# Weight splitting in a fused two-block transformer: one block per run of matmuls in the attention layers, and every low part issued one block behind its high part

## The chip, the cores and the metric

The kernel runs on one core of one Trainium2 chip. The metric is the time of one execution in device microseconds (us). Instructions of one engine run in the order in which they stand in that engine's queue; PE is TensorE (matmuls), DVE is VectorE, ACT is ScalarE, POOL is GpSimd, SP is the queue that issues most of the loads.

## What is computed

The reference runs two model blocks, one behind the other, on 256 tokens of width 1024 in fp32. Cut to what matters:

```python
def first_block(x, mem, ...):                    # two layers
    mem_n = rmsnorm(mem, mem_norm_g)
    for i in range(2):
        mem_k, mem_v = split(mem_n @ mem_w_kv[i])
        x = x + 0.5 * swiglu(rmsnorm(x, norm_g[i, 0]), ffn_w_up[i, 0], ffn_w_down[i, 0])
        h = rmsnorm(x, norm_g[i, 1])
        x = x + (pool_layer(h, ...) if i == 0 else diff_layer(h, ...))
        x = x + 0.5 * swiglu(rmsnorm(x, norm_g[i, 2]), ffn_w_up[i, 1], ffn_w_down[i, 1])
    return rmsnorm(x, final_norm_g)

def second_block(x, c, ...):                     # one layer
    mod = silu(c) @ w_ada + b_ada                # six vectors of shifts, scales and gates
    h = modulate(rms_norm(x, norm_attn), sh1, sc1)
    x = x + g1 * hybrid_mixer(h, w_in, w_out, rel_bias)   # MOBA heads and DSA heads (top-k select)
    h = modulate(rms_norm(x, norm_ffn), sh2, sc2)
    x = x + g2 * peer_ffn(h, w_query, sub_keys, u_emb, v_emb)   # 16384 experts, top 16 of 8 heads
    return rms_norm(x, norm_final)
```

`pool_layer` mixes moving averages with attention over `mem`; `diff_layer` is causal attention with the difference of two softmaxes, beside attention over `mem`.

## The kernel before, in words

**Products in three matmuls.** Each fp32 operand is split into a high part (rounded to the matmul's fp32r format) and a low part (the rest). A product is the sum of high x high (L184), high x low (L185) and low x high (L186), which `mm3` issues one after the other for each 128 rows of the inner dimension.

**Weights as a stream.** All weights come as 654 blocks of up to 512 KB, here counted 0 to 653 in the order in which they are used. For each block SP issues a load into a `raw` buffer (five buffers, later four), ACT copies it into `whi` (L144), and DVE subtracts into `wlo` (L145). In between lie items with a `call`: pieces of the matrix `w_ada`, which DVE adds up itself (`ada_piece`, the rows `acc` of L463 and L465) beside the feed-forward halves.

```python
    def split_one():
        j = st["split"]
        load_to(j + cfg["raw"])
        ...
            ACT.activation(hi[:, :n], r[:, :n], AF.Copy)
            V.tensor_tensor(lo[:, :n], r[:, :n], hi[:, :n].bitcast(F32), op=OP.subtract)
```

**When a block is split.** The tile framework's scheduler is off: the order of the program is the order of each engine. A group of matmuls begins with `fetch(4)`, which calls `nextw` for each of the four blocks that the group uses, and `nextw` splits until four blocks beyond the one that it hands out are split (`cfg["ahead"]` is 4; 2 for the experts). So the four blocks of the next group are split at the start of this one, in a row on ACT and on DVE.

**Where the blocks are used.** 0 to 15 are the keys and values of `mem`; 16 to 81, 108 to 173, 174 to 239 and 280 to 345 the four feed-forward halves (44 blocks up, 22 down); 82 to 107 the pool layer; 240 to 279 the diff layer; 346 to 381 the projections of MOBA and DSA; 382 to 397 the query projection of the experts, 398 to 653 the experts. In the up projections a group is 4 blocks by 96 matmuls of 128x256: the weights are stationary, and the first 24 matmuls go through all four blocks once, so the group meets its fourth block's low part at its 21st matmul.

**Layers with other work between.** In the attention layers generators are stepped in turn: `proj_cols`, `v_part` or `u_part` (one run of matmuls to a step), and units of attention, whose steps put softmax rows on DVE and ACT and small matmuls and transposes on PE. A table `counts` sets how many runs of matmuls follow each step. The output projection of the hybrid attention (`out_proj_k`) calls `fetch(4)` for blocks 382 to 385 and then `realT(0)`, which computes the modulation `ma` (L343), scales the transposed activations (`xg`, L355 and L353) and splits them into `hT` for the next projection.

Of the kernel before, what the change touches and what calls it, by code (L numbers as in the profile page):

```python
# [60 lines left out]
def kernel(ctx: ExitStack, tc: tile.TileContext, A, LAY, stop=None):  # L61
# [4 lines left out]
    def pool(name, bufs=1, **kw):  # L66
        return tc.tile_pool(name=name, bufs=bufs, reuse_waits="tile", **kw)
# [32 lines left out]


    items = []
    st = {"load": 0, "split": 0, "use": 0, "nsplit": 0, "raw": {}, "s": {}}
    deferred = []
    cfg = {"raw": 5, "ahead": 4}
    CH = 1024
    wpool = ctx.enter_context(pool("wp", side="right"))
    wstack = ctx.enter_context(ExitStack())
# [11 lines left out]
    def load_to(n):  # L120
        while st["load"] < min(n, len(items)):
            ap, nk, w = items[st["load"]][:3]
            if st["load"] < dense and st["load"] % 5 == 4:
                r = wpool2.tile([P, CH], F32, name="raw", tag="raw", bufs=1)
            else:
                r = wpool.tile([P, CH], F32, name="raw", tag="raw", bufs=4)
            nc.sync.dma_start(r[:, :nk * w], ap)
            st["raw"][st["load"]] = r
            st["load"] += 1

    def split_one():
        j = st["split"]
        load_to(j + cfg["raw"])
        _, nk, w, call = items[j][:4]
        n = nk * w
        r = st["raw"].pop(j)
        if call is not None:
            call(r[:, :n].rearrange("p (k w) -> p k w", w=w))
        else:
            p_ = wpool2 if j < dense and st["nsplit"] % 2 else wpool  # L140
            st["nsplit"] += 1
            hi = p_.tile([P, CH], F32R, name="whi", tag="whi", bufs=4)
            lo = p_.tile([P, CH], F32R, name="wlo", tag="wlo", bufs=4)
            ACT.activation(hi[:, :n], r[:, :n], AF.Copy)  # L144
            V.tensor_tensor(lo[:, :n], r[:, :n], hi[:, :n].bitcast(F32), op=OP.subtract)  # L145
            st["s"][j] = Split(hi[:, :n].rearrange("p (k w) -> p k w", w=w), lo[:, :n].rearrange("p (k w) -> p k w", w=w))
        st["split"] += 1
        load_to(j + 1 + cfg["raw"])

    def nextw():  # L150
        while items[st["use"]][3] is not None:
            st["use"] += 1
        j = st["use"]
        ahead, k = 0, j + 1
        while k < len(items) and ahead < cfg["ahead"]:
            ahead += items[k][3] is None
            k += 1
        while st["split"] < k:
            split_one()
        st["use"] += 1  # L160
        return st["s"].pop(j), items[j][1], items[j][2]

    def split_more(n):
        for _ in range(n):
# [12 lines left out]
    def run_deferred():  # L177
        while deferred:
            deferred.pop(0)()
        for f in strip_hook:  # L180
            f()
# [21 lines left out]
    def rows_mm(p, act, got, t, c0, w, K):  # L203
        for c, k, kt in got:
            mm3(p, act[:, kt, t * P:(t + 1) * P], c[:, k, c0:c0 + w], kt == 0, kt == K - 1)
# [18 lines left out]
    def proj_cols(act, n, n_ct, evac):  # L224
        got = fetch(n)
        for c0 in range(0, n_ct, 2):
            p = pmm()
            m = min(2, n_ct - c0)
            for j in range(m):
                if j:  # L230
                    yield
                proj_col(act, got, c0 + j, p[:, j * S:(j + 1) * S])
            evac(c0, m, p[:, :m * S].rearrange("p (j t) -> p j t", t=S))
            yield
        run_deferred()

    def drain(*gens):
        for g in gens:
            for _ in g:
                pass  # L240
# [153 lines left out]
    def out_proj_k(segs, update, nxt, tail=2, ahead=None):  # L394


        p = [[pmm() for _ in range(2)] for _ in range(NT)]
        n = len(segs)

        def mm(t, h, gis, gots):  # L400
            for gi in gis:
                act, k0 = segs[gi]
                for c, k, _ in gots[gi][h]:
                    mm3(p[t][h], act[:, k0 + k, t * P:(t + 1) * P], c[:, k, :], gi == 0 and k == 0, gi == n - 1 and k == 1)

        gots = {}
        for gi in range(n - tail):
            gots[gi] = [fetch(1), fetch(1)]
            for t in range(NT):
                for h in range(2):  # L410
                    mm(t, h, [gi], gots)
                if t:
                    run_deferred()
                yield
        was = dict(cfg)
        cfg.update(ahead=8 - 2 * tail)
        for gi in range(n - tail, n):
            gots[gi] = [fetch(1), fetch(1)]
        cfg.update(was)
        for t in range(NT):  # L420
            for h in range(2):
                cut = n - 1 if nxt.deep and t and h else n
                mm(t, h, range(n - tail, cut), gots)
                if cut < n:
                    was = dict(cfg)
                    cfg.update(ahead=0)
                    ahead.append(fetch(4))
                    nxt.realT(0)
                    mm(t, h, range(cut, n), gots)
                    if tail > 2:  # L430
                        split_more(1)
                update(t, h, p[t][h])
                nxt.pre(t, h)
                if not nxt.deep and (t or h):
                    nxt.T(*((0, 0), (0, 1), (1, 0))[2 * t + h - 1])
                if h:
                    nxt.stats(t)
                if cut < n:
                    ahead.append(fetch(4))
                    cfg.update(was)  # L440
                yield
        if not nxt.deep:
            nxt.late = [lambda: nxt.T(1, 1)]
# [306 lines left out]
        return dump(xt)  # L750

    n2 = Norm(A["norm_g"][0, 2])
    with pool("pl") as sp:
        cat = Split(sp.tile([P, 12, S], F32R, name="cat_hi"), sp.tile([P, 12, S], F32R, name="cat_lo"))
        pb = sp.tile([P, 4, 384], F32, name="poolB")
# [6 lines left out]
        def u_part(h):  # L762
            got = fetch(4)
            for t in range(NT):
                n1.before(t)
                p = pmm()
                rows_mm(p, hT, got[:4], t, 0, 512, 8)
                yield
                rows_mm(p, hT, got[4:], t, 0, 512, 8)
                ACT.activation(u[t][:, h * 512:(h + 1) * 512], p, AF.Copy, scale=n1.rstd[:, t:t + 1])  # L770
                if t:
                    run_deferred()
                yield

        def pooled(c0):
# [8 lines left out]
        def mixed():  # L784
            for c0 in range(0, 8, 2):
                pooled(c0)
                yield
            wg = fetch(2)
            for ct in range(8):
                g, db = ct // 2, ct % 2  # L790
                p = psm()[:, :S]
                for cb in range(2):
                    col = cb * S + db * P
                    mm3(p, wg[g][0][:, g % 2, col:col + P], hT[:, 2 * g + cb, :], cb == 0, cb == 1)
                split_evac(cat[:, ct, :], p, psc[:, ct:ct + 1])
                if ct % 2:
                    yield

        drain(u_part(0), proj_cols(hT, 4, 4, lambda c0, m, p: ACT.activation(qT[:, c0:c0 + m, :], p, AF.Copy)))
# [3 lines left out]
        for n, _ in zip(counts, pipeline(units, [(1, 2), (3, 3), (None, 0), (0, 0), (2, 2)])):  # L803
            for _ in range(n):
                step(fill)
        drain(fill)
    kv0.close()
    if stop == "pool":
        return dump(xt)
# [9 lines left out]


    n5 = Norm(A["norm_g"][1, 2])
    with pool("df") as sp:
        cat = Split(sp.tile([P, 12, S], F32R, name="cat_hi"), sp.tile([P, 12, S], F32R, name="cat_lo"))
        nd = sp.tile([P, S], F32, name="nd")
# [97 lines left out]
        def v_part(h):  # L922

            got = fetch(4)
            for t in range(NT):
                n4.before(t)
                p = pmm()
                rows_mm(p, hT, got[:4], t, 0, 512, 8)
                yield
                rows_mm(p, hT, got[4:], t, 0, 512, 8)  # L930
                ACT.activation(v[:, t, h * 512:(h + 1) * 512], p, AF.Copy, scale=n4.rstd[:, t:t + 1])
                if t:
                    run_deferred()
                yield

        drain(v_part(0))
# [12 lines left out]
        for i, _ in enumerate(pipeline(units, [(5, 6), (1, 2), (4, 4), (None, 0), (6, 6), (0, 0), (3, 3), (2, 2)])):  # L949
            for _ in range(counts[i] if i < len(counts) else 1):  # L950
                step(fill)
        drain(o)
    kv1.close()
    if stop == "diff":
        return dump(xt)
# [45 lines left out]
        return dump(xt)  # L1001


    gotv, got = m1.got
    mvp = [pmm() for _ in range(NT)]
    iqp, ixp = pmm(), psm()
# [93 lines left out]
    def v_part():  # L1100
        got = fetch(4)
        for t in range(NT):
            p = pmm()
            rows_mm(p, hT, got[:4], t, 0, 512, 8)
            yield
            rows_mm(p, hT, got[4:], t, 0, 512, 8)
            ACT.activation(av[:, t, 512:], p, AF.Copy)
            if t:
                run_deferred()
            yield  # L1110

    def make(t, g):
# [88 lines left out]
        return dump(xt)  # L1201


    got = m2.got
    def q_rows(b, t):
        p = pmm()
# [87 lines left out]
    for f in late_scores:  # L1294
        f()
    q1st.close()
    wstack.close()
    pq2 = pqst.enter_context(pool("pq2"))

# [335 lines left out]
```

## Time and profile before

| what | value |
|---|---|
| time, median of 3 runs | 2098.37 us (2098.26 to 2100.83) |
| the profiled execution: time, span of its instructions | 2098.71 us, 2096.9 us |
| mean granted clock of TensorE | 0.987 |
| PE busy | 2033.5 us, 97% of the span |
| DVE busy | 1458.4 us, 70% |
| ACT busy | 985.5 us, 47% |

The profile is of one execution. Busy time is the time in which an engine has an instruction under way; the granted clock is TensorE's clock as a share of its full 2.4 GHz. A row of the timeline gives the start and duration in us, the engine, the line, the operation, what is written `<-` what is read, the size, how many like instructions in a row (x4), and in brackets the idle time of the engine ahead of it with what ended it.

### The profile page before, as it was taken

The page shows a single profiled execution, that of the slowest core. Times are in us where ns is not written, and L with a number is a line of the kernel's source. Part 1 is how long each engine was busy: PE and PEld are TensorE (multiplying, and loading weights), DVE is VectorE, ACT ScalarE, POOL GpSimd, SP SyncE. Part 2 cuts the span into 40 slices and gives each one's busy share as a digit, 9 for nine tenths or more (in the row PEclk, how much of TensorE's full clock was granted, in tenths as well). Part 3 has the DMA queues.
Part 4 walks back from the last instruction along what each step waited for, and adds up shares of the span by engine and source line. Part 5 has one row for each costly group of instructions (what it writes and reads, how often), then busy time and mean ns, then how long its engine had stood idle before and what let it go on. Part 6 is the DMA issues. An engine that isn't in the chain of part 4 may idle for free. (4 is left out here: it accounts for less than half of the span.)

```text
span 2096.9 us, 34488 instructions
## 1 busy us (share of the span) xinstructions
PE 2033.5 (97%) x13678; PEld 1832.0 (87%) x13678; DVE 1458.4 (70%) x2330; ACT 985.5 (47%) x1508; POOL 39.0 (2%) x74
## 2 busy tenths in 40 slices
PE   8999999999999998899989899999999999999998
PEld 7999888998999797799878779999998888888886
DVE  6677566776677568756658688889976666666666
ACT  6444454444444445354444344455554444444444
POOL 2000000000000000000000000000000000000000
PEclk9999999999999999999999899999999999999999
DMA  7667535676576552355545333556676776777764
GB/s 274 217 236 266 188 134 205 227 250 233 185 248 244 187 195 101 120 191 198 206 124 180 104 98 134 175 178 213 245 252 209 226 231 207 225 243 225 225 211 140
DMA packets 142379, 416.93 MB, mean 199 GB/s; under 512 B 12469, under 2 KB 47429, under 8 KB 140041
## 3 DMA queue, kind: packets, MB, share of 16 engines
q1 hardware_dynamic: 102672, 372.04, 52.4%
q10 hardware_dynamic: 37976, 36.91, 5.5%
q0 software_dynamic: 1568, 5.77, 0.9%
q8 instruction: 107, 1.75, 0.3%
q14 instruction: 56, 0.45, 0.1%
HBM read 396.82 MB, written 17.86 MB: 198 GB/s over the span
## 5 line engine op out<-in xcount | busy, mean ns | idle before, releaser
L145 DVE TENSOR_TENSOR wlo<-raw,whi 128x1024 fp32r<-128x1024 f32 (+1 forms) x654 | 780.6, 1222 | 329.8 <-ACT whi L144 329.5
L144 ACT ACTIVATE whi<-raw 128x1024 fp32r<-128x1024 f32 (+1 forms) x654 | 663.0, 1048 | 147.6 <-PE mm L186 85.4
L184 PE MATMUL mm<-hT_hi,whi 128*128 128x256 f32 x1680 | 479.9, 286 | 0.0
L185 PE MATMUL mm<-hT_lo,whi 128*128 128x256 f32 x1680 | 473.1, 282 | 0.0
L186 PE MATMUL mm<-hT_hi,wlo 128*128 128x256 f32 x1680 | 472.9, 281 | 0.0
L184 PEld LDWEIGHTS mm<-hT_hi,whi 128*128 128x128 f32 x1680 | 319.0, 190 | 6.5 <-issue 6.1
L185 PEld LDWEIGHTS mm<-hT_lo,whi 128*128 128x128 f32 x1680 | 318.9, 190 | 2.0 <-issue 1.9
L186 PEld LDWEIGHTS mm<-hT_hi,wlo 128*128 128x128 f32 x1680 | 318.7, 190 | 0.0
L184 PE MATMUL sm<-hT_hi,whi 128*128 128x256 f32 (+1 forms) x1048 | 299.5, 286 | 5.4 <-DVE hT_hi L192 2.2
L186 PE MATMUL sm<-hT_hi,wlo 128*128 128x256 f32 (+1 forms) x1048 | 296.5, 283 | 4.4 <-DVE wlo L145 4.4
L185 PE MATMUL sm<-hT_lo,whi 128*128 128x256 f32 (+1 forms) x1048 | 296.1, 283 | 0.4 <-DVE hT_lo L195 0.4
L184 PEld LDWEIGHTS sm<-hT_hi,whi 128*128 128x128 f32 (+1 forms) x1048 | 199.2, 190 | 8.7 <-DVE hT_hi L192 2.6
L184 PE MATMUL mm<-whi,wh 128*128 128x512 f32 x512 | 204.1, 399 | 2.1 <-ACT wh L194 2.1
L186 PEld LDWEIGHTS sm<-hT_hi,wlo 128*128 128x128 f32 (+1 forms) x1048 | 199.2, 190 | 4.8 <-DVE wlo L145 4.8
L186 PE MATMUL mm<-whi,wl 128*128 128x512 f32 x512 | 202.2, 395 | 0.0
L185 PEld LDWEIGHTS sm<-hT_lo,whi 128*128 128x128 f32 (+1 forms) x1048 | 199.3, 190 | 2.8 <-DVE hT_lo L195 0.6
L185 PE MATMUL mm<-wlo,wh 128*128 128x512 f32 x512 | 201.5, 394 | 0.0
L194 ACT ACTIVATE wh<-wf 128x256 fp32r<-128x256 f32 x128 | 53.5, 418 | 215.6 <-DVE wf L1484 215.6
L184 PE MATMUL mm<-whi,gT_hi 128*128 128x512 f32 x352 | 140.0, 398 | 0.0
L186 PE MATMUL mm<-whi,gT_lo 128*128 128x512 f32 x352 | 139.5, 396 | 0.0
L185 PE MATMUL mm<-wlo,gT_hi 128*128 128x512 f32 x352 | 138.6, 394 | 0.0
L1316 ACT ACTIVATE act<-sm 128x256 f32<-128x256 f32 x128 | 49.1, 384 | 166.3 <-PE sm L186 166.3
(308 smaller groups left out, 2615.9 us busy)
## 6 DMA issues: line engine op xcount, KB each, us to landing
raw<-in_ffn_up_dram SPq DMA_DIRECT2D x176, 512.0 KB, 5.2
raw<-in_peer_u_dram SPq DMA_DIRECT2D x128, 512.0 KB, 3.7
raw<-in_peer_v_dram SPq DMA_DIRECT2D x128, 512.0 KB, 3.8
raw<-in_ffn_dn_dram SPq DMA_DIRECT2D x88, 512.0 KB, 5.2
raw<-in_w_ada_dram SPq DMA_DIRECT2D x48, 512.0 KB, 5.0
gall<-stage ACTq DMA_DIRECT2D x16, 1024.0 KB, 4.6
G<-gall ACTq DMA_DIRECT2D x16, 1024.0 KB, 7.2
raw<-in_diff_w_in_dram SPq DMA_DIRECT2D x28, 512.0 KB, 5.5
```

Of the source, the lines that this page charges most:

```text
L144: ACT.activation(hi[:, :n], r[:, :n], AF.Copy)
L145: V.tensor_tensor(lo[:, :n], r[:, :n], hi[:, :n].bitcast(F32), op=OP.subtract)
L184: PE.matmul(out, a[0], b[0], start=start, stop=False)
L185: PE.matmul(out, a[0], b[1], start=False, stop=False)
L186: PE.matmul(out, a[1], b[0], start=False, stop=stop)
L194: ACT.activation(hi, src, AF.Copy)
L1316: ACT.activation(act[n], p, AF.Gelu)
```

## The change

`split_one` no longer issues the low part. It appends the block to a list, and `low_one` issues the subtraction on DVE when the next block's high part has been issued (so one low part is always pending), ahead of going on after a `call` item (behind that item's own rows), or when `nextw` hands out a block whose low part is still missing. In the pool layer, the diff layer and the hybrid attention `cfg["spread"]` is set: there `nextw` splits no further than the block that it hands out, and `ahead_one`, called after each run of matmuls, splits one block if fewer than four beyond those handed out are split. Loads are issued later by as many blocks as low parts are pending.

```diff
+    def low_one():
+        j, r, p_ = st["low"].pop(0)
+        c = st["s"][j]
...
+        V.tensor_tensor(lo[:, :nk * w], r[:, :nk * w], c.hi.rearrange("p k w -> p (k w)").bitcast(F32), op=OP.subtract)
...
     def split_one():
...
-        load_to(j + cfg["raw"])
+        load_to(j + cfg["raw"] - len(st["low"]))
...
             ACT.activation(hi[:, :n], r[:, :n], AF.Copy)
-            V.tensor_tensor(lo[:, :n], r[:, :n], hi[:, :n].bitcast(F32), op=OP.subtract)
...
+            st["low"].append((j, r, p_))
         st["split"] += 1
-        load_to(j + 1 + cfg["raw"])
+        while len(st["low"]) > 1 or st["low"] and call is not None:
+            low_one()
+        load_to(j + 1 + cfg["raw"] - len(st["low"]))

     def nextw():
...
-        while k < len(items) and ahead < cfg["ahead"]:
+        while k < len(items) and ahead < cfg["ahead"] and not cfg["spread"]:
             ahead += items[k][3] is None
             k += 1
         while st["split"] < k:
             split_one()
+        while st["s"][j].lo is None:
+            low_one()
...
+    def ahead_one():
+        if cfg["spread"] and st["split"] < min(st["use"] + 4, len(items)):
+            split_one()
...
     def proj_cols(act, n, n_ct, evac):
...
                 if j:
+                    ahead_one()
                     yield
                 proj_col(act, got, c0 + j, p[:, j * S:(j + 1) * S])
             evac(c0, m, p[:, :m * S].rearrange("p (j t) -> p j t", t=S))
+            ahead_one()
             yield
```

`ahead_one()` stands likewise ahead of the yields of `u_part`, `v_part`, `mixed` and `out_proj_k`. PE's instructions keep their order. On ACT and DVE nothing is added or removed; the splitting rows alone move among the others.

At the very start, DVE's queue holds the transposed `mem` (`xg`, scaled; `mT_lo`, its low parts) and the low parts of blocks 0 to 3. Before:

```order
L680 TENSOR_TENSOR xg<-tr,cols 128x512 x2
L145 TENSOR_TENSOR wlo<-raw,whi 128x1024
L683 TENSOR_TENSOR mT_lo<-xg,mT_hi 128x4x128
L680 TENSOR_TENSOR xg<-tr,cols 128x512
L683 TENSOR_TENSOR mT_lo<-xg,mT_hi 128x4x128
L680 TENSOR_TENSOR xg<-tr,cols 128x512
L683 TENSOR_TENSOR mT_lo<-xg,mT_hi 128x4x128 x2
L145 TENSOR_TENSOR wlo<-raw,whi 128x1024 x3
```

Now (the same rows have other line numbers, L703 for L680, L706 for L683, L137 for L145):

```order
L703 TENSOR_TENSOR xg<-tr,cols 128x512 x2
L706 TENSOR_TENSOR mT_lo<-xg,mT_hi 128x4x128
L703 TENSOR_TENSOR xg<-tr,cols 128x512
L706 TENSOR_TENSOR mT_lo<-xg,mT_hi 128x4x128
L703 TENSOR_TENSOR xg<-tr,cols 128x512
L706 TENSOR_TENSOR mT_lo<-xg,mT_hi 128x4x128 x2
L137 TENSOR_TENSOR wlo<-raw,whi 128x1024 x4
```

The low part of block 0 went from ahead of all `mT_lo` to behind them.

In the up projection of the first feed-forward half, DVE's queue around the start of the group that uses blocks 28 to 31; `gate` is the previous group's last product, `acc` a piece of `w_ada`, `wlo_948` the low part of block 31. Before, with buffer numbers:

```order
L532 TENSOR_TENSOR gate_921<-mm_872,silu_784 128x512
L145 TENSOR_TENSOR wlo_926<-raw_789,whi_925 128x1024
L465 SCALAR_TENSOR_TENSOR acc_797<-raw_795,cols_79,acc_797 128x512 x2
L145 TENSOR_TENSOR wlo_936<-raw_800,whi_935 128x1024
L145 TENSOR_TENSOR wlo_942<-raw_806,whi_941 128x1024
L145 TENSOR_TENSOR wlo_948<-raw_812,whi_947 128x1024
```

Now block 31's low part is `wlo_1058`, and stands one group further back:

```order
L530 TENSOR_TENSOR gT_lo_694<-tr_862,gT_hi_693 128x512
L530 TENSOR_TENSOR gT_lo_694<-gate_917,gT_hi_693 128x512
L555 TENSOR_TENSOR gate_1052<-mm_1003,silu_920 128x512
L488 SCALAR_TENSOR_TENSOR acc_793<-raw_931,cols_79,acc_793 128x512 x2
L137 TENSOR_TENSOR wlo_1058<-raw_925,whi_943 128x1024
L137 TENSOR_TENSOR wlo_1068<-raw_933,whi_1064 128x1024
```

It was issued a whole group of matmuls ahead of its use and is now issued in the group that uses it, behind that group's `gate` and two `acc` rows.

At the end of the hybrid attention, DVE's queue from the residual's update (`x_66`, the second half of the tokens) to the next projection's input (`hT`). Before:

```order
L1031 TENSOR_TENSOR x_66<-x_66,xg 128x512
L343 SCALAR_TENSOR_TENSOR ma<-mod,cols 128x8
L355 TENSOR_SCALAR xg<-tr,ma,mod 128x128 x4
L192 CAST hT_hi<-xg 128x4x128
L195 TENSOR_TENSOR hT_lo<-xg,hT_hi 128x4x128 x2
```

Now:

```order
L1064 TENSOR_TENSOR x_66<-x_66,xg 128x512
L137 TENSOR_TENSOR wlo<-raw,whi 128x1024 x4
L363 SCALAR_TENSOR_TENSOR ma<-mod,cols 128x8
L375 TENSOR_SCALAR xg<-tr,ma,mod 128x128 x4
L210 CAST hT_hi<-xg 128x4x128
L213 TENSOR_TENSOR hT_lo<-xg,hT_hi 128x4x128 x2
```

The low parts of blocks 382 to 385, which stood some 10 rows earlier, now stand between the update and `ma`; on ACT their high parts stand likewise ahead of the other half of `xg` (L353).

## Rows read from the trace of the kernel before

**Rows 1.** The page: PE's part of the first section, and the low parts' group.

```profile
PE 2033.5 (97%) x13678; PEld 1832.0 (87%) x13678; DVE 1458.4 (70%) x2330; ACT 985.5 (47%) x1508; POOL 39.0 (2%) x74
...
L145 DVE TENSOR_TENSOR wlo<-raw,whi 128x1024 fp32r<-128x1024 f32 (+1 forms) x654 | 780.6, 1222 | 329.8 <-ACT whi L144 329.5
```

**Rows 2.** PE's waits: what waited for what, us in total, times, longest.

```profile
PE tr L243 <- DVE cat_lo L201: 5.1, 2, 4.3
PE tr L243 <- DVE rc L867: 4.6, 1, 4.6
...
PE sm L186 <- DVE wlo L145: 4.4, 2, 3.9
PE tr L243 <- DVE e L1152: 3.8, 1, 3.8
PE tr L243 <- DVE xscale L561: 2.8, 1, 2.8
PE sm L1124 <- DVE e L1130: 2.4, 1, 2.4
...
PE sm L1124 <- DVE yA_lo L195: 2.0, 1, 2.0
PE sm L1124 <- DVE hT_lo L195: 1.8, 1, 1.8
...
PE sm L184 <- DVE cat_lo L201: 1.7, 2, 1.5
```

**Rows 3.** Stretches behind four of PE's waits: length, PE busy, granted clock, DMA.

```profile
302.83:306.83 4.00, 3.81 (x30) 1.00 0.64 231
...
822.70:826.70 4.00, 4.00 (x23) 0.62 0.68 257
...
1172.96:1180.96 8.00, 8.00 (x34) 0.57 0.47 169
...
1215.40:1219.40 4.00, 4.00 (x9) 0.50 0.58 195
```

**Rows 4.** Timeline of the diff layer, PE at one row, then DVE.

```profile
812.79 0.28 PE L186 MATMUL mm<-hT_hi,wlo 128*128 128x256 f32 x1
...
815.51 0.17 DVE L249 TENSOR_SCALAR ms<-oss 128x4 f32<-128x4 f32 x1 [0.85 <-ACT junk L253]
816.47 4.63 DVE L145 TENSOR_TENSOR wlo<-raw,whi 128x1024 fp32r<-128x1024 f32 x4 [0.78 <-ACT whi L144]
821.01 0.74 DVE L198 TENSOR_SCALAR cat_hi<-tr,sng 128x512 fp32r<-128x512 f32 x1
```

**Rows 5.** Timeline of the first feed-forward half: PE at block 31, and DVE.

```profile
96.95 0.28 PE L186 MATMUL mm<-hT_hi,wlo 128*128 128x256 f32 x1
...
95.74 1.53 DVE L465 SCALAR_TENSOR_TENSOR acc<-raw,cols,acc 128x512 f32<-128x512 f32 x2
```

**Rows 6.** Timeline of the start: PE at blocks 0 and 7, and DVE.

```profile
11.53 0.63 PE L185 MATMUL mm<-wlo,mT_hi 128*128 128x512 f32 x1
...
12.42 1.47 DVE L683 TENSOR_TENSOR mT_lo<-xg,mT_hi 128x512 fp32r<-128x512 f32 x2
...
26.25 0.28 PE L186 MATMUL mm<-mT_hi,wlo 128*128 128x256 f32 x1
...
27.96 0.15 DVE L249 TENSOR_SCALAR ms<-ss 128x1 f32<-128x1 f32 x1
```

**Rows 7.** Timeline of the top-k select: PE at block 361, and DVE.

```profile
1134.90 0.28 PE L186 MATMUL mm<-hT_hi,wlo 128*128 128x256 f32 x1
...
1130.23 0.29 DVE L1090 MAX8 m<-score 128x8 f32<-128x128 f32 x1
...
1136.21 0.41 DVE L1091 MATCH_REPLACE8 score<-m,score 128x256 f32<-128x256 f32 x1
```

**Rows 8.** Timeline of the end of the hybrid attention, DVE and PE.

```profile
1243.56 0.69 DVE L1031 TENSOR_TENSOR x<-x,xg 128x512 f32<-128x512 f32 x1
1244.17 0.16 DVE L343 SCALAR_TENSOR_TENSOR ma<-mod,cols 128x8 f32<-128x8 f32 x1
...
1246.32 0.50 PE L184 MATMUL mm<-whi,hT_hi 128*128 128x512 f32 x1 [0.78 <-DVE hT_hi L192]
```

More of the change, by code (lines that the diff above doesn't have):

```diff
@@ L102 @@
     items = []
-    st = {"load": 0, "split": 0, "use": 0, "nsplit": 0, "raw": {}, "s": {}}
+    st = {"load": 0, "split": 0, "use": 0, "nsplit": 0, "raw": {}, "s": {}, "low": []}
     deferred = []
-    cfg = {"raw": 5, "ahead": 4}
+    cfg = {"raw": 5, "ahead": 4, "spread": False}
     CH = 1024
@@ L129, in load_to @@
             st["load"] += 1
+    def low_one():
+        j, r, p_ = st["low"].pop(0)
+        c = st["s"][j]
+        nk, w = items[j][1:3]
+        lo = p_.tile([P, CH], F32R, name="wlo", tag="wlo", bufs=4)
+        V.tensor_tensor(lo[:, :nk * w], r[:, :nk * w], c.hi.rearrange("p k w -> p (k w)").bitcast(F32), op=OP.subtract)
+        c.lo = lo[:, :nk * w].rearrange("p (k w) -> p k w", w=w)
     def split_one():
         j = st["split"]
-        load_to(j + cfg["raw"])
+        load_to(j + cfg["raw"] - len(st["low"]))
         _, nk, w, call = items[j][:4]
@@ L142, in split_one @@
             hi = p_.tile([P, CH], F32R, name="whi", tag="whi", bufs=4)
-            lo = p_.tile([P, CH], F32R, name="wlo", tag="wlo", bufs=4)
             ACT.activation(hi[:, :n], r[:, :n], AF.Copy)
-            V.tensor_tensor(lo[:, :n], r[:, :n], hi[:, :n].bitcast(F32), op=OP.subtract)
-            st["s"][j] = Split(hi[:, :n].rearrange("p (k w) -> p k w", w=w), lo[:, :n].rearrange("p (k w) -> p k w", w=w))
+            st["s"][j] = Split(hi[:, :n].rearrange("p (k w) -> p k w", w=w), None)
+            st["low"].append((j, r, p_))
         st["split"] += 1
-        load_to(j + 1 + cfg["raw"])
+        while len(st["low"]) > 1 or st["low"] and call is not None:
+            low_one()
+        load_to(j + 1 + cfg["raw"] - len(st["low"]))
     def nextw():
@@ L413, in out_proj_k @@
                     run_deferred()
+                ahead_one()
                 yield
@@ L440, in out_proj_k @@
                     cfg.update(was)
+                if not nxt.deep:
+                    ahead_one()
                 yield
@@ L752 @@
     n2 = Norm(A["norm_g"][0, 2])
+    cfg["spread"] = True
     with pool("pl") as sp:
@@ L767, in u_part @@
                 rows_mm(p, hT, got[:4], t, 0, 512, 8)
+                ahead_one()
                 yield
@@ L772, in u_part @@
                     run_deferred()
+                ahead_one()
                 yield
@@ L796, in mixed @@
                 if ct % 2:
+                    ahead_one()
                     yield
@@ L806 @@
         drain(fill)
+    cfg["spread"] = False
     kv0.close()
@@ L821 @@
     n5 = Norm(A["norm_g"][1, 2])
+    cfg["spread"] = True
     with pool("df") as sp:
@@ L928, in v_part @@
                 rows_mm(p, hT, got[:4], t, 0, 512, 8)
+                ahead_one()
                 yield
@@ L933, in v_part @@
                     run_deferred()
+                ahead_one()
                 yield
@@ L952 @@
         drain(o)
+    cfg["spread"] = False
     kv1.close()
@@ L1001 @@
         return dump(xt)
+    cfg["spread"] = True
     gotv, got = m1.got
@@ L1104, in v_part @@
             rows_mm(p, hT, got[:4], t, 0, 512, 8)
+            ahead_one()
             yield
@@ L1109, in v_part @@
                 run_deferred()
+            ahead_one()
             yield
@@ L1201 @@
         return dump(xt)
+    cfg["spread"] = False
     got = m2.got
@@ L1296 @@
     q1st.close()
+    while st["low"]:
+        low_one()
     wstack.close()
```

## The prediction

> **What bounds the kernel now.** I read the page first: PE is busy for 2033.5 of 2096.9 us, so the kernel is a nearly closed chain of matmuls, and an edit pays only through PE's idle time (63 us, the start's wait for the first load among it) or its clock. DVE waits 329.5 us for high parts ahead of low parts [rows 1], but nearly all of that lies under PE's work and is worth nothing by itself. PE's waits say where it is worth something: eight kinds of wait in the attention layers, 24.2 us in all, are for DVE rows (softmax weights `e`, `cat_lo`, `hT_lo`, `yA_lo`, small factors) [rows 2]. In the timeline at each of them the same picture: two to four low parts in a row stand ahead of the wanted row, as the 4.63 us ahead of `cat_hi` [rows 4], often after a wait for a high part. Then I read windows behind the waits: after 4.3 and 3.8 us of idleness the granted clock falls to the 1.2 GHz level, mean 0.62 over 4 us and 0.57 over 8 us, so 1.5 and 3.4 us more are lost; behind the 1.8 us it falls too (0.50 over 4 us), behind a wait of 1.5 us it stays at 1.00 [rows 2, 3].
>
> Then, for all 654 blocks, I set two times side by side: when PE first uses the low part, and when DVE gets to it in the changed order, which is the end of the row now ahead of it plus the low parts between (1.14 us each in a row, (4.63 - 1.22) / 3 [rows 4], the last 1.22 [rows 1]). Where the second is later, PE stands: PE is in order, and so is DVE.
>
> **The change part by part.** *What it removes.* In the attention layers at most two low parts, and no wait for a fresh high part, are left ahead of the wanted rows. Of the 24.2 us [rows 2] I leave 2.4 (0.8 of the 2.8 for `xscale`, 0.7 of the 1.8 for `hT_lo`, 0.2 to 0.4 of three others): gain 21.8 us. Three smaller waits, and DVE's pace in the last six experts, where the low part no longer waits for its high part: 3.0. Seven falls of the clock go with these waits: six of about 1.7 (0.50 to 0.62 over 4 us) and one of 3.4: 13.7. Sum of gains: 38.5 us. If other rows then come last, half of that is the lower bound.
>
> *What it adds at the start.* Block 0's low part stands behind all `mT_lo`, the last of which ends at 12.42 + 1.47 = 13.89; it is ready at 15.1, and PE wants it at 11.53: 3.6 us. Block 7's stands behind `ms<-ss`, which ends at 28.11: ready at 29.3, wanted at 26.25: 3.1 us [rows 6]. The rows ahead of it wait for the normalisation's squares on ACT, queued there behind an eviction that waits for PE; so the second delay comes on top of the first. Together 6.7, nothing hides it: no other work of PE is ready.
>
> *In the feed-forward halves* nothing is spread, but each low part is one place later. The last of four goes from the group ahead into the group that uses it, and PE comes to it 2.34 us after the group's start. Where a piece of `w_ada` lies between, two `acc` rows go first: they end at 95.74 + 1.53 = 97.27, the low part at 98.49, wanted at 96.95: 1.5 us [rows 5]. Nine groups have this (three in each of the first three halves), by the same subtraction between 1.1 and 1.5: 11.4 us. Each stays under the gap that costs the clock. The other up groups have 0.2 to 0.4 us to spare, taken as nothing (at worst 2 us). Down groups have over 1 us.
>
> *In the layers with spread* `nextw` forces the last low part of a group at its `fetch`, wherever DVE's queue stands. Three places are large. Block 267: behind `ms<-oss`, which ends at 815.68; ready at 816.9, wanted at 812.79: 4.1 us [rows 4]. Block 361, in the top-k select: two steps of the select last 1136.62 - 1130.23 = 6.39, and low parts now stand ahead of, between and behind them: 1130.23 + 1.14 + 6.39 + 1.14 + 1.22 = 1140.1, wanted at 1134.90: 5.2 us [rows 7]. Blocks 382 to 385: DVE's four low parts (4.63) and the wait for the first high part (about 1.0, it follows the squares of x on ACT) come between the update of x and `ma`, and PE waits for what follows: 5.6 us more than the 0.78 of now [rows 8]. Nine smaller ones, between 0.6 and 2.3 (block 259, behind softmax rows), make 9.7. Four gaps (blocks 7, 267, 361, 382) are long enough for a fall of the clock, at 1.7 each: 6.8; with 3.4 each it would be 13.6.
>
> *The experts.* In the route stage DVE is busy throughout, and blocks 393 and 397 get their low parts one top-16 job later; PE then waits there in place of the 3.9 us at block 400 [rows 2]. What is left over, some 2 us, falls ahead of two later waits for the stage that DVE bounds. I take nothing; bounds -3 and +4. In the steady stream PE finds its low part 0.1 to 0.7 us early in place of 2.6: nothing. Loads start one block later, 2.8 us of several that a raw block lies ready; nothing.
>
> *Sum.* Losses 6.7 + 11.4 + (4.1 + 5.2 + 5.6) + 9.7 + 6.8 = 49.5; gains 38.5; net +11.0. Against the profiled execution's own 2098.71 us that is 2109.7; it lies 0.3 above the median of the runs, so 2109.4, said as 2109. Bounds of the unknown clock (+6.8), the small waits (-9.7) and the experts (-3, +4) give this forecast 2099 to 2120, and 2101 to 2117 as its likely range.
>
> By the Trainium skill, "TensorE: Matmul & The Clock Gate", section "A second HAM failure mode: psum-queue depth-cycling", a PE that idles for short times between groups of matmuls, often enough, has its clock swing between both levels and loses throughput to that. So far the trace does not bear it out here: a single gap of 1.5 us left the clock at 1.00.
>
> **Rivals.** *A, faster: DVE comes to the late low parts earlier than I reckon.* The row ahead of them is itself queued behind low parts that are now gone; where DVE was full (the select, the diff layer) it moves up by 1.14 for each, and the squares or softmax sums may follow. For: DVE has 329.5 us of waits less to stand in. Against: the rows ahead of blocks 267 and 382 wait for ACT or PE, not DVE. If the late parts of the spread layers (14.9 + 7.9 of the small ones) and their three falls (5.1) go, 2109.4 - 27.9 = 2081.5 us. It decides if the lateness at 267 and 382 falls under 1 us.
>
> *B, no change: the feed-forward stalls are not there*, because the `gate` row ahead, and so `acc`, starts sooner. For: DVE is idle for a while ahead of it. Against: `gate` reads the group's last sum, so it can't. 2109.4 - 11.4 = 2098.0 us.
>
> *C, slower still: short gaps cost the clock* (the page's rule as a mechanism). Eighteen gaps of 0.6 to 2.3 us, in groups 35 us apart, each with a fall at 1.7 us: 2109.4 + 30.6 = 2140 us. Against it the stretch behind the 1.5 us [rows 3].
>
> That the change does nothing is excluded: ACT's and DVE's orders differ at nearly every block.
>
> **How the numbers follow.** Forecast 0.62, A 0.14, B 0.16, C 0.08. No change means within 0.2%, 4.2 us of 2098.4, about what a measurement of this kernel can tell. Of the forecast's own range 0.04 lies within it, of B's spread a quarter on either side (0.04 faster, 0.08 same, 0.04 slower): faster 0.14 + 0.04 = 0.18, same 0.12, slower 0.70. The range leaves out C and most of A: 2092 to 2121.
>
> **What would show it.** Right: PE's waits list `wlo` as what it waits for, at 11.5 and 26 us, nine times some 1.1 to 1.5 us in the up projections, and 4 to 5 us in the diff layer and the select; `ma` preceded by four low parts and a PE gap near 6 us; the waits for `rc`, `e`, `yA_lo` gone, and with them the stretches of half clock there. Wrong: if PE's idle time falls below 63 us, A holds; if `wlo` waits in the up projections are missing, B; if the mean clock falls below 0.98 while the gaps are as said, C.

## The result, and the profile after

The changed kernel takes 2124.27 us (median of 4 runs, 2122.10 to 2128.06) against 2098.32 before: 26 us or 1.2% slower, ratio 1.0124, 95% interval 1.0106 to 1.0142. Two executions in all the runs told here, at 4715.55 and 4997.97 us, took more than twice the time and are left out of every median and ratio. The forecast was 11 us slower, with 2121 as the upper end of its range. The profiled execution took 2122.99 us, its span is 2121.2, and the mean granted clock is 0.987 as before.

The page of the changed kernel: PE's part of the first section, and the groups of the low and high parts.

```profile
PE 2037.2 (96%) x13678; PEld 1831.8 (86%) x13678; DVE 1442.1 (68%) x2330; ACT 983.2 (46%) x1508; POOL 44.8 (2%) x74
...
L137 DVE TENSOR_TENSOR wlo<-raw,whi 128x1024 fp32r<-128x1024 f32 (+1 forms) x654 | 778.8, 1219 | 127.2 <-ACT whi L153 126.7
L153 ACT ACTIVATE whi<-raw 128x1024 fp32r<-128x1024 f32 (+1 forms) x654 | 669.3, 1049 | 183.4 <-DMA raw<-in_ffn_up_dram 68.7
```

Against [rows 1] DVE's wait for high parts fell from 329.5 to 126.7 us, and the kernel is slower all the same: PE's idle time rose from 63.4 to 84.0 us. That wait lay under PE's work, and its size said nothing about the time. What counts is PE's list of waits:

```profile
PE mm L204 <- DVE wlo L137: 31.7, 25, 4.5
PE mm L202 <- DVE hT_hi L210: 10.8, 2, 7.1
...
PE mm L203 <- DVE wlo L137: 7.8, 4, 3.2
PE sm L204 <- DVE wlo L137: 4.8, 5, 1.8
PE tr L263 <- DVE e L901: 2.3, 1, 2.3
```

The softmax rows and factors of [rows 2] are nearly gone from it; in their place PE waits 44.3 us for low parts, 34 times. Each place that the prediction named is there. The start, block 0 behind `mT_lo` and block 7 behind `ms` [rows 6]:

```profile
12.45 1.47 DVE L706 TENSOR_TENSOR mT_lo<-xg,mT_hi 128x512 fp32r<-128x512 f32 x2
13.84 2.35 DVE L137 TENSOR_TENSOR wlo<-raw,whi 128x1024 fp32r<-128x1024 f32 x2
...
15.11 0.80 PE L203 MATMUL mm<-wlo,mT_hi 128*128 128x512 f32 x1 [3.22 <-DVE wlo L137]
...
32.24 0.15 DVE L269 TENSOR_SCALAR ms<-ss 128x1 f32<-128x1 f32 x1
32.31 3.48 DVE L137 TENSOR_TENSOR wlo<-raw,whi 128x1024 fp32r<-128x1024 f32 x3
...
33.58 0.58 PE L204 MATMUL mm<-mT_hi,wlo 128*128 128x256 f32 x1 [2.87 <-DVE wlo L137]
```

Block 31 in the first up projection [rows 5], one of nine alike (0.99 to 1.02 us):

```profile
104.72 1.53 DVE L488 SCALAR_TENSOR_TENSOR acc<-raw,cols,acc 128x512 f32<-128x512 f32 x2
106.17 2.35 DVE L137 TENSOR_TENSOR wlo<-raw,whi 128x1024 fp32r<-128x1024 f32 x2
...
107.44 0.39 PE L204 MATMUL mm<-hT_hi,wlo 128*128 128x256 f32 x1 [1.02 <-DVE wlo L137]
```

Blocks 267, 361 and 382 to 385, in the diff layer, the select and the end of the hybrid attention [rows 4, 7, 8]:

```profile
847.61 0.17 DVE L269 TENSOR_SCALAR ms<-oss 128x4 f32<-128x4 f32 x1 [0.85 <-ACT junk L273]
847.69 2.35 DVE L137 TENSOR_TENSOR wlo<-raw,whi 128x1024 fp32r<-128x1024 f32 x2
...
848.97 0.58 PE L204 MATMUL mm<-hT_hi,wlo 128*128 128x256 f32 x1 [4.51 <-DVE wlo L137]
...
1163.78 1.22 DVE L137 TENSOR_TENSOR wlo<-raw,whi 128x1024 fp32r<-128x1024 f32 x1
...
1165.05 0.58 PE L204 MATMUL mm<-hT_hi,wlo 128*128 128x256 f32 x1 [3.31 <-DVE wlo L137]
...
1260.28 0.69 DVE L1064 TENSOR_TENSOR x<-x,xg 128x512 f32<-128x512 f32 x1
1262.77 4.63 DVE L137 TENSOR_TENSOR wlo<-raw,whi 128x1024 fp32r<-128x1024 f32 x4 [1.80 <-ACT whi L153]
1267.32 0.16 DVE L363 SCALAR_TENSOR_TENSOR ma<-mod,cols 128x8 f32<-128x8 f32 x1
...
1269.56 0.77 PE L202 MATMUL mm<-whi,hT_hi 128*128 128x512 f32 x1 [7.12 <-DVE hT_hi L210]
```

Two kinds of place were forecast too small or not at all. One is the first group of the feed-forward halves behind the pool and the diff layer: the low parts of blocks 110 and 111 (282 and 283) stand behind the last `ms` of the layer, and PE stands 2.02 us, twice. The other is in the diff layer: DVE's low part at 833.34 waits for its high part, which ACT (busy until then with another unit's rows) has only just done, and the `e` row behind it is late. First the pool layer's end, then the diff layer:

```profile
361.12 0.15 DVE L269 TENSOR_SCALAR ms<-ss 128x1 f32<-128x1 f32 x1
361.19 3.48 DVE L137 TENSOR_TENSOR wlo<-raw,whi 128x1024 fp32r<-128x1024 f32 x3
...
362.46 0.50 PE L203 MATMUL mm<-wlo,hT_hi 128*128 128x512 f32 x1 [2.02 <-DVE wlo L137]
...
833.34 1.23 DVE L137 TENSOR_TENSOR wlo<-raw,whi 128x1024 fp32r<-128x1024 f32 x1 [2.92 <-ACT whi L153]
...
836.16 0.74 PE L263 MATMUL tr<-ident,e 128*128 128x128 f32 x4 [2.27 <-DVE e L901]
```

Since PE's order is the same, the gap ahead of each can be subtracted, one by one, and so can its start time (its shift). In gaps alone, without what the clock does behind them:

| term | forecast, us | gaps of the profiled executions, us |
|---|---|---|
| start, blocks 0 and 7 | +6.7 | +6.1 |
| nine feed-forward groups | +11.4 | +9.0 |
| 267, 361, 382 to 385 | +14.9 | +14.2 |
| other new waits ahead of the experts (0.25 us and more) | +9.7, nine of them | +16.7, eighteen of them |
| waits that go or shrink, the experts left out | -24.8 | -27.2 |
| experts (new 9.4, gone 7.7) | 0 | +1.7 |
| all gaps | +17.9 | +20.6 |
| clock, and what else is not a gap | -6.9 | +3.7 |
| sum | +11.0 | +24.3 |

The last row is the difference of the two profiled executions; the medians differ by 26.0, by which the row above it would be +5.4. The forecast's 24.8 holds a share for DVE's pace in the last experts that it doesn't give apart; the measured 27.2 leaves the experts out.

### The profile page after: what moved, and what is told of

The parts are those of the page before. It is cut to its first block, busy times and chain, and to the rows that moved or that the text cites. A ratio compares the mean times of both kernels' runs of the same rounds, so it can differ in the third digit from the quotient of the medians.

```text
span 2121.2 us, 34238 instructions
## 1 busy us (share of the span) xinstructions
PE 2037.2 (96%) x13678; PEld 1831.8 (86%) x13678; DVE 1442.1 (68%) x2330; ACT 983.2 (46%) x1508; POOL 44.8 (2%) x74
## 4 chain that ended last, share of the span: by engine, by line
PE 84%; DVE 11%; ACT 2%; issue 1%; DMA 1%; ACTq 0%; POOL 0%; DVEq 0%; POOLq 0%; SPq 0%
PE mm L204 21%; PE mm L202 21%; PE mm L203 21%; PE sm L204 5%; PE sm L202 5%; PE sm L203 5%; DVE wlo L137 4%; PE mm L1472 2%; PE tr L263 1%; ACT junk L273 1%; DVE i L1266 1%; ACT whi L153 0%; DVE v L1264 0%; DMA mem<-in_mem_dram 0%; DVE e L879 0%
## 5 line engine op out<-in xcount | busy, mean ns | idle before, releaser
L137 DVE TENSOR_TENSOR wlo<-raw,whi 128x1024 fp32r<-128x1024 f32 (+1 forms) x654 | 778.8, 1219 | 127.2 <-ACT whi L153 126.7
L153 ACT ACTIVATE whi<-raw 128x1024 fp32r<-128x1024 f32 (+1 forms) x654 | 669.3, 1049 | 183.4 <-DMA raw<-in_ffn_up_dram 68.7
L213 DVE TENSOR_TENSOR wl<-wf,wh 128x256 fp32r<-128x256 f32 x128 | 54.5, 426 | 198.3 <-ACT wh L212 198.3
```

The source lines that it names most:

```text
L137: V.tensor_tensor(lo[:, :nk * w], r[:, :nk * w], c.hi.rearrange("p k w -> p (k w)").bitcast(F32), op=OP.subtract)
L213: V.tensor_tensor(lo, src, hi.bitcast(F32), op=OP.subtract)
```

## Experiments

First theory, T: the loss is the sum of single waits for low parts that stand behind rows which themselves wait; each place that is mended gives its own part back. Rivals: S, the spreading itself costs, and the lateness little; L, loads issued one block later starve ACT (its waits for `raw` of the up projections rose to 68.7 us); W, the waits are conserved, and where one late row is mended another takes over. All ratios are against the kernel before, with their 95% intervals. What one version gains over another is the difference of their medians; the kernel before itself moved by 1 us from round to round (2098.3 to 2099.4).

**The two halves of the change, apart.** Low parts at once, spreading kept:

```diff
-        while len(st["low"]) > 1 or st["low"] and call is not None:
+        while st["low"]:
             low_one()
```

> The changed kernel, but each low part is issued at once behind its own high part; the spreading over the runs of matmuls stays. Theory T (the loss is low parts that stand one block late, behind rows of DVE that wait): block 0 and block 7 at the start (9.4 us with the slow matmuls behind them), the nine groups of the feed-forward halves (11.0), blocks 259, 267 and 361 with their falls of the clock (some 5, 6.2 and 5.5) and half of what blocks 110, 111, 282 and 283 cost come back; 382 to 385, whose high and low parts still stand between x and ma, stay. 2124 - 9.4 - 11.0 - 16.7 - 4 = 2083, range 2076 to 2092 us, faster than the kernel before. Rival S (the spreading itself costs, by its waits for fresh high parts, and the lateness little): above 2110 us. Rival L (loads issued one block later starve ACT): the loads are as early here as before, so it too expects 2083 or so; another run tells it apart.

Measured: 2125.16 us, 1.0128 (1.0113 to 1.0144). T's number fails by 42 us; S's range (above 2110) is where it lands. At the start and in the nine groups the late low parts are indeed gone (shift +0.3 us at 50 us), but the spread layers are far worse than before: the shift grows by 4.6 us in the pool layer and 8.4 in the diff layer, where the changed kernel gains 3.0. A low part at once behind its own high part makes DVE wait for ACT, in front of softmax rows, at many of the splits. DVE's waits in this kernel, over the diff layer's stretch (750 to 895 us) and over 1125 to 1225 us in the hybrid attention:

```profile
DVE wlo L137 <- ACT whi L153: 22.7, 15, 4.0
...
DVE wlo L137 <- ACT whi L153: 19.2, 10, 3.5
```

The kernel before has 5.2 and 5.1 us there: 4 and 3 low parts wait, against 15 and 10 here. So spreading by itself is a loss here; it needs the lag.

Lag kept, spreading off (each of the three assignments of True):

```diff
-    cfg["spread"] = True
+    cfg["spread"] = False
```

> The changed kernel without the spreading: blocks are split four at a time everywhere as in the kernel before, but each low part is issued one block behind its high part, and loads one block later. T: the start (9.4 us) and the nine feed-forward groups (11.0) are lost as in the changed kernel, some 1 to 3 us more where a last low part is forced at the end of a layer, and the waits of the attention layers stay: 2098 + 9.4 + 11.0 + 2 = 2120, range 2116 to 2124 us. S: the lateness costs little, 2098 to 2106. L: as T, since the loads are late here too.

Measured: 2107.41 us, 1.0040 (1.0026 to 1.0054), 13 us better than T's number, and just outside S's range (2098 to 2106); L, which expected the same as T, misses with it. Start and feed-forward halves cost as expected (shifts +5.9 and +11.3), but the lag alone already gains 10.2 us in the hybrid attention and 1.8 in the diff layer. What the two halves do in each stretch, beside the changed kernel (change of PE's shift, us, against the kernel before, in profiled executions):

| stretch | changed | at once | lag only | three repairs | until next block | until third run |
|---|---|---|---|---|---|---|
| start, to 50 us | +9.3 | +0.3 | +5.9 | -0.5 | +0.4 | +0.1 |
| feed-forward halves, first groups apart | +12.2 | +1.7 | +11.3 | -0.4 | +1.1 | -0.7 |
| pool layer | -0.1 | +4.6 | -0.8 | -0.2 | -0.8 | -1.9 |
| diff layer | -3.0 | +8.4 | -1.8 | -2.8 | -1.5 | -4.8 |
| first groups (110, 282) | +7.7 | +4.4 | 0.0 | -0.1 | -0.1 | 0.0 |
| hybrid attention, ahead of 382 | -9.2 | +0.8 | -10.2 | -9.8 | -10.0 | -8.9 |
| 382 to 385 | +6.4 | +6.0 | +0.9 | +0.9 | +0.9 | +0.9 |
| query projection and experts | +1.0 | +0.7 | +6.1 | +2.0 | +1.8 | +0.6 |
| sum | +24.3 | +26.9 | +11.5 | -10.8 | -8.1 | -14.7 |

The last three columns are runs told below.

**Loads.** The kernel before, with every load one block later:

```diff
-        load_to(j + cfg["raw"])
+        load_to(j + cfg["raw"] - 1)
...
-        load_to(j + 1 + cfg["raw"])
+        load_to(j + cfg["raw"])
```

> The kernel before, with each load issued one block later and nothing else changed (high and low parts stay where they were). T: the raw blocks still lie ready before ACT wants them nearly everywhere: 2098 to 2101 us. L (late loads starve ACT, whose waits for raw blocks grew from 8 to 69 us in the changed kernel): 2112 to 2122 us.

Measured: 2100.20 us, 1.0009 (1.0000 to 1.0018): 2 us at most come from issuing the loads later. This run does not bring back ACT's long waits, though: for `raw` of the up projections ACT waits 10.0 us in it, 8.4 in the kernel before and 68.7 in the changed one. That those waits are under cover too is seen in the kernel with the three repairs below, in which ACT still waits 65.9 us there and PE for none of the up projections' low parts. With both, L falls.

**One place mended at a time**, in the changed kernel. Ahead of a piece of `w_ada`:

```diff
         if call is not None:
+            while st["low"]:
+                low_one()
             call(r[:, :n].rearrange("p (k w) -> p k w", w=w))
```

> The changed kernel, but a pending low part is issued ahead of the rows of a piece of w_ada instead of behind them; nothing else moves. T: the nine waits of the up projections (1.0 us each, 11.0 us in the shift of PE's instructions) go, all other losses stay: 2124 - 11 = 2113, range 2111 to 2115 us. L (late loads): the high parts come no earlier, PE still waits, 2120 to 2124. S: no change, 2124.

Measured: 2114.57 us, 1.0082 (1.0069 to 1.0095): 9.7 us come back, and the nine waits are gone. The start:

```diff
     split_one()
+    low_one()
     for h in range(2):
...
     split_more(4)
+    low_one()
```

> The changed kernel, but at the start the low part of block 0 is issued right behind its high part, and that of block 7 right behind its own, as in the kernel before; nothing else moves. T (each late low part costs PE its own wait, and the costs add up): the shift at 50 us, 9.3 in the changed kernel's profile and 5.9 and 6.0 in two others with the same start, goes: 2124 less 6 to 9 is 2115 to 2118 us. Rival W (the waits are conserved: where one late row is mended, the next row that comes late takes over): less than half comes back, 2120 to 2124 us.

Measured: 2115.89 us, 1.0081 (1.0068 to 1.0094): 8.4 us come back. The last groups of the output projections:

```diff
-        cfg.update(ahead=8 - 2 * tail)
+        cfg.update(ahead=8 - 2 * tail, spread=False)
```

> The changed kernel, but in the last groups of the output projections the blocks are split ahead in one go, as in the kernel before, still with the low part one block behind: blocks 110, 111, 282 and 283 get their low parts ahead of the update of x, and three of the four low parts of 382 to 385 leave the place between x and ma. T: the two groups at the start of the feed-forward halves give back 3.8 and 3.9 us, 382 to 385 some 5 of their 6.1: 2124 - 13 = 2111, range 2109 to 2114 us. W: 2117 to 2124 us.

Measured: 2111.33 us, 1.0056 (1.0043 to 1.0069): 12.9 us come back; both first groups are at 0.0 in the shift, and 382 to 385 at +0.9 in place of +6.4. All three together:

> The changed kernel with three repairs together: low part ahead of the pieces of w_ada, the start as before, the last groups of the output projections split in one go. T: the three gains add up, 9.7 as measured for the first, 6 to 9 and 13: 2124 - 30 = 2094, range 2090 to 2097 us, a little faster than the kernel before. W: 2105 us and more.

Measured: 2089.26 us, 0.9962 (0.9948 to 0.9976), 10 us faster than the kernel before. The single gains are 31.0, together 35.0: they add up, and W falls for these places. How this kernel comes to be faster than the one before is seen on its page:

```profile
PE 2022.6 (97%) x13678; PEld 1820.4 (87%) x13678; DVE 1442.8 (69%) x2330; ACT 982.9 (47%) x1508; POOL 42.4 (2%) x74
```

Its span is 2086.2 us, so PE is idle for 63.6 us, as in the kernel before (63.4). The waits have moved and not shrunk. What fell is PE's busy time, by 10.9 us, and the mean granted clock of this execution is 0.995 in place of 0.987: in this execution the gain lies in the clock and not in PE's idle time.

**The attention layers.** A version with the lag in the three attention layers alone, no spreading, and the pending low part issued after the next run of matmuls:

```diff
-        while len(st["low"]) > 1 or st["low"] and call is not None:
+        while len(st["low"]) > cfg["lag"] or st["low"] and call is not None:
...
     def ahead_one():
-        if cfg["spread"] and st["split"] < min(st["use"] + 4, len(items)):
-            split_one()
+        if st["low"]:
+            low_one()
```

> What the runs so far point to: the low part one block behind only in the three attention layers, at once elsewhere (start, feed-forward, experts); no spreading, blocks are split four at a time as in the kernel before; a low part still pending is issued after the next run of matmuls. T: of the lateness alone the run had -0.8 in the pool layer, -1.8 in the diff layer with a wait of 3.7 at block 267 in it that now goes, and -10.2 in the hybrid attention with 4 at blocks 361 and 365 that go: 2098 - 1 - 5 - 14 = 2078, range 2073 to 2085 us. W: 2090 us and more.

Measured: 2099.26 us, 0.9997 (0.9987 to 1.0008): nothing is left of the gain, and T's 2078 fails by 21. In the four low parts that DVE issues in a row the last one is back in front of the same softmax rows as in the kernel before, and PE's four waits between 800 and 900 us are the old ones (5.1 for `cat_lo`, 4.6 and 1.3 for `rc`, 2.8 for `xscale`). The same without that early issue (the pending low part stays until the next block is split or wanted):

> As the last one (low parts one block behind in the attention layers alone, no spreading), but a pending low part is not issued after the next run of matmuls; it stays until the next block is split or wanted. In DVE's order only one row in each group moves: of the four low parts in a row ahead of a softmax row, the last, which waits for a high part that ACT has only just been given, is replaced by one whose high part is long done. Theory Q (what the change gains in the attention layers is DVE's wait for that freshest high part, not the number of low parts in a row, and the spreading adds nothing): the shifts by layer of the run with the lateness alone, -0.8, -1.8 and -10.2, with +0.9 at 382 to 385: 2099 - 12 = 2087, range 2083 to 2091 us. Rival N (it was the lateness together with the loads or the later layers): 2095 to 2099 us as the run before.

Measured: 2088.38 us, 0.9952 (0.9938 to 0.9967), as Q said; N falls. How it gains is seen ahead of `rc` in the diff layer. The kernel with the early issue, then this one:

```profile
838.29 2.36 DVE L137 TENSOR_TENSOR wlo<-raw,whi 128x1024 fp32r<-128x1024 f32 x2 [3.52 <-ACT whi L153]
...
841.17 0.16 DVE L894 RECIPROCAL rc<-sum 128x2 f32<-128x2 f32 x1
```

```profile
833.12 1.22 DVE L137 TENSOR_TENSOR wlo<-raw,whi 128x1024 fp32r<-128x1024 f32 x1
836.73 1.23 DVE L137 TENSOR_TENSOR wlo<-raw,whi 128x1024 fp32r<-128x1024 f32 x1 [2.39 <-ACT whi L153]
...
838.47 0.16 DVE L896 RECIPROCAL rc<-sum 128x2 f32<-128x2 f32 x1
```

Two low parts stand there in both; but in the second kernel the first is an old one, whose high part is long done, and it runs while DVE waits for ACT anyway: the wait shrinks by 1.13 us (3.52 to 2.39), and PE's wait for `rc` from 4.56 to 3.43. So Q is half right: not the whole wait goes, only one low part's time of it.

Two versions that issue the pending low part after the second and the third run of matmuls (`st["age"]` counts them):

```diff
-        if st["low"]:
+        st["age"] += 1
+        if st["low"] and st["age"] >= 2:
             low_one()
```

> As the kernel with the pending low part left until the next block, but it is issued after the second run of matmuls behind its high part at the latest. Q: by then the high part is done, so the gain of the attention layers stays, and the low parts of blocks 267, 361 and 365 come two runs earlier than forced, so PE's waits for them (3.9, 2.2 and 1.5 us with one fall of the clock each at the first two) go: 2087 - 9 = 2078, range 2074 to 2083 us. Rival M (any low part that is issued between the units' rows stands in front of a softmax row): 2088 to 2099 us.

> As before, with the third run of matmuls in place of the second. Q: the same 2078, range 2074 to 2085 us, since the high part is done by then and most forced low parts still come earlier. M: 2085 to 2095 us, nearer to the kernel that leaves it until the next block.

Measured: 2089.42 us, 0.9960 (0.9946 to 0.9975), and 2084.80 us, 0.9934 (0.9920 to 0.9947). With the third run the time lies at the edge of both ranges, Q's and M's. With the second it lies in M's range and Q misses by 11 us; what is left of PE's waits between 800 and 900 us shows why:

```profile
PE tr L265 <- DVE cat_lo L221: 5.1, 2, 4.3
PE tr L265 <- DVE rc L897: 3.4, 1, 3.4
PE tr L265 <- DVE xscale L585: 1.6, 1, 1.6
PE tr L265 <- DVE rc L595: 0.2, 1, 0.2
```

PE no longer waits for block 267, but the 4.3 us for `cat_lo` [rows 2] are back in full. In the two kernels in which they are gone, the changed one and the one that leaves the low part until the next block, PE has just stood 4.5 and 3.9 us at block 267. So there W holds: PE waits in one place or in the other. The waits that do shrink here do so by 1.13 to 1.14 us (`rc` twice, `xscale`), one low part each. With the third run `cat_lo` shrinks by 1.14 too, and in the select PE waits 1.8 us for a low part in place of 2.4 for `e`. This is the fastest kernel of the study. Its gaps do not explain all of it: in its profiled execution PE's last matmul comes 14.7 us earlier than before, and the gaps shrink by 8.3. The rest is again clock. Behind the wait for `hT_lo`, for one, which is down from 1.8 to 0.6 us, 4 us at 0.50 [rows 3] have become (PE busy, granted clock, DMA)

```profile
1201.45:1205.45 4.00, 4.00 (x18) 1.00 0.41 131
```

and the matmuls behind it come another 3 us earlier.

Last, the three repairs with low parts at once behind the last attention layer (query projection and experts):

> The changed kernel with the three repairs, and low parts at once behind the last attention layer (query projection and experts). T: what the late low parts of blocks 393, 397 and the experts cost (3.2 + 0.6 - 1.8 us in the shifts, against 0.9 - 1.2 with low parts at once) goes: 2089 - 2 = 2087, range 2084 to 2090 us. If it is as fast as the kernel with the lateness alone in the attention layers, the spreading adds nothing (Q).

Measured: 2088.74 us (five executions), 0.9955 (0.9939 to 0.9971). By the medians that is 0.5 us from the three repairs alone, too little to tell, though its trace has 1.6 us less shift in the query projection and the experts. And it is as fast as the lag in the attention layers alone (2088.38): spreading adds nothing that can be measured to the lag, as Q said.

## Why the prediction was wrong

The direction was right, and so was the mechanism of the losses: every named place stands in PE's list of waits, and mending the places gives their time back one by one. Two terms of the sum failed, both mostly on the side of the losses.

**The clock is the larger one.** The step was "Four gaps (blocks 7, 267, 361, 382) are long enough for a fall of the clock, at 1.7 each: 6.8", against 13.7 of falls that go: net -6.9. The measured net is +3.7 us. Behind it stood a reading of [rows 2, 3], where 1.5 us left the clock up and 1.8 us did not, as if the length of a gap decided ("Each stays under the gap that costs the clock"); the last section shows that it doesn't. By stretches (shift less gaps): the diff layer and the hybrid attention gave back 7.7 net, with the new falls at 267 and 361 in it (forecast 13.7 - 3.4 = 10.3), but the start lost 3.8 in place of 1.7, and the two first groups, for which no fall was in the sum, lost 3.6. 382 to 385 lost the 1.7 forecast. The nine short waits lost 2.0 us more than their gaps: PE's next matmuls came 1.1 to 1.3 us later for each gap of 1.0, with the granted clock at 1.00 over the 4 us behind all nine, so this part isn't clock; with it, the 11.4 forecast for them came out (11.0), though the gaps themselves were shorter.

**The small waits are the other.** "Nine smaller ones, between 0.6 and 2.3 ..., make 9.7" became eighteen with 16.7 us. Of these, 4.0 are the two first groups (2.02 each) and 3.3 two rows of the diff layer, `e` at 836 us (2.27) and `xscale` (0.98), that the low parts of the changed order make late. Of its nine the prediction names only block 259, so which of the eighteen it had can't be told. It searched for low parts that come late for PE, and held that "no wait for a fresh high part" is left ahead of the wanted rows. But a low part that waits for one makes the row behind it late as well, as the 2.92 us at 833 us did for `e`, and such rows were not searched for.

**What held.** Start 6.7 against 6.1; the three large ones 14.9 against 14.2, in part by luck, since one by one they are 4.5, 3.3 and 6.3 against 4.1, 5.2 and 5.6; waits gone 24.8 against 27.2; experts 0 against 1.7, within their bounds. That the loads cost next to nothing was shown by the run with late loads and by the three repairs. Two small slips, seven falls that add up to 13.6 and not 13.7 and a lower bound that adds up to 2097 and not 2099, matter for nothing. Rival A (DVE comes earlier) falls by its own sign: PE stands 4.5 us at block 267 and 6.3 us more ahead of 382 to 385. B falls: the nine waits are there. C falls as it was put: behind the nine gaps of 1.0 us the clock stayed; but behind the two of 2.02 us it fell. The rule of the Trainium skill that was weighed there ("TensorE: Matmul & The Clock Gate", section "A second HAM failure mode: psum-queue depth-cycling"), by which short idle times between groups of matmuls, repeated often enough, cost the clock, is not borne out by the nine gaps of 1.0 us. They lie some 35 us apart; gaps in quicker succession were not tried.

**A reason that was wrong without showing.** The gain was put down to both halves, at most two low parts and no wait for a fresh high part ahead of the wanted rows. The runs show that the lag alone does it, at about 1.1 us of wait a place and, as far as the traces tell, as much again in falls of the clock that no longer come; that the rest of what vanished was exchanged for waits at blocks 267, 361 and 365; and that the spreading alone loses 27 us.

## What to carry to other kernels

When work is deferred on an in-order engine, list for every deferred row the rows that now stand ahead of it and what those wait for, and do the same for the rows behind it; layer ends, where a reduction waits for another engine, were among the dearest places. A wait that a change removes is only worth what isn't waited for elsewhere on the same engine: take the two together before adding both. Add up idle time and granted clock apart: one kernel here gained 10 us with as much idle time as before. Test the halves of a change apart early: here one half was a loss of 27 us by itself, and the other, kept to the layers that gain from it, was 0.4 to 0.7% faster than the kernel before.

## What the runs showed of the hardware

The length of a gap did not decide whether the granted clock fell to the 1.2 GHz level behind it. Windows of 4 us behind gaps in the changed kernel: 1.02 us (a feed-forward group), 2.27 us (`e`), 2.02 us (block 110) and 3.31 us (block 361). The clock is the number behind POOL's:

```profile
107.44:111.44 4.00, 4.00 (x34) 4.00 (x35) 2.22 (x2) 0.88 (x1) 0.00 (x0) 1.00 0.67 235
...
836.16:840.16 4.00, 4.00 (x20) 3.02 (x22) 3.93 (x14) 2.33 (x10) 1.05 (x1) 1.00 0.30 112
...
362.46:366.46 4.00, 4.00 (x13) 3.08 (x14) 4.00 (x4) 2.07 (x3) 0.89 (x2) 0.67 0.68 212
...
1165.00:1169.00 4.00, 3.95 (x18) 3.95 (x19) 3.79 (x13) 0.00 (x0) 0.00 (x0) 0.50 0.40 131
```

A gap of 2.27 us left it at 1.00, one of 2.02 brought it to 0.67, and in the kernel before one of 1.8 us had brought it to 0.50 [rows 3]. And the same gap of 2.01 us ahead of block 110, in the kernel with the start mended:

```profile
352.57:356.57 4.00, 4.00 (x19) 3.31 (x20) 4.00 (x4) 2.10 (x3) 0.88 (x2) 1.00 0.57 194
```

There the clock stayed at 1.00, and the shift behind it is 2.2 us instead of 3.8. The gap of 2.9 us at block 7 did likewise. In the changed kernel:

```profile
33.58:37.58 4.00, 4.00 (x18) 0.50 0.73 245
```

(PE busy, granted clock, DMA). Of the three other kernels with the same start the one with the last groups mended has 0.57 there, and the ones with the lag alone and with the low part ahead of the pieces of `w_ada` have 1.00; the shifts at 50 us are 9.3 and 8.8 against 5.9 and 6.0 us. So a fall behind a gap of some 2 to 3 us is neither sure nor excluded, and cost 1.6 to 3.4 us in these places where it came. What decides it, no run here tells.
